# The opening of a two-layer decoder trunk: first loads in turns, the first chunk in four banks, TensorE on constants

## The chip, the cores and the metric

The kernel runs on one core of one Trainium2 chip, as one launch. The metric is the device time of that launch in microseconds (us). The kernel before takes 2181.18 us, the median of three runs (2179.99 to 2181.38).

A core has five engines that run their own instruction streams and meet at semaphores: TensorE (PE; its weight loads, PEld, are shown apart), VectorE (DVE), ScalarE (ACT), GpSimd (POOL) and SyncE (SP), which here only issues transfers. The transfers of all queues run on the same 16 DMA engines.

## The reference, cut to what matters

```python
DEPTH = 2; SEQ = 256; D_MODEL = 2048; PROJ_WIDTH = 6144
def reference(x, w_in, w_out, ...):
    for l in range(DEPTH):
        h = _rmsnorm(x, attn_norm_g[l])
        proj = h @ w_in[l]
        q, k, v, gate_b, gate_c, conv_in = jnp.split(proj, splits, axis=-1)
        q = _rmsnorm(q.reshape(B, S, N_HEADS, 2, HEAD_DK), q_norm_g[l])
        k = _rmsnorm(k.reshape(B, S, N_HEADS, 2, HEAD_DK), k_norm_g[l])
        ...
        attn = _diff_attention(q, k, v, lam, rel_bias)
        ...
        conv = gate_b * _short_conv(gate_c * conv_in, conv_w[l])
        x = x + jnp.concatenate([attn, conv.astype(attn.dtype)], axis=-1) @ w_out[l]
        hm = _rmsnorm(x, mlp_norm_g[l]) @ w_up[l]
        x = x + jnp.square(jax.nn.relu(hm)) @ w_down[l]
    return x
```

The change touches the first step of the first layer: x (256 rows of 2048) is loaded, turned, scaled by the gain of the norm, and multiplied with the first 512 columns of `w_in` (the first half of q). The row factor of the norm is applied later, to the product.

## The kernel before

**Numbers in two parts.** All large products are done in TensorE's reduced float32 (FP32R), with each operand split in two: a rounded high part (`hi`), made by ScalarE, and the rest (`lo`), made by VectorE from the original and the high part. Three products (high x high, high x low, low x high; `TERMS`, line 38) stand for one. So each weight tile that arrives as `raw` costs one ScalarE instruction (L282) and one VectorE instruction (L283) before TensorE can use it, and so does each piece of turned x (`split_gained`, L248 and L249, which also multiplies by the gain).

**Tiling.** x lies in four chunks `xs[n]` of 512 columns, each with both blocks of 128 rows. A chunk holds four K tiles of 128 columns. `Norm.chunk` turns a chunk with TensorE (L402): two banks of the accumulator memory, each with two K tiles of 256 rows, then four `split_gained` into the tile `nT`, then two squares on ScalarE with a running sum (L412), from which `Norm.factors` makes the row factors when all four chunks are ready. `linear` (L325) walks over 16 K tiles; for each it does six matmuls of 512 columns (two row blocks, three terms) against 512 columns of weights. Weights come two K tiles at a time, 512 KB, through four raw buffers and three buffers each for `hi` and `lo`.

**Order.** TensorE's instructions run in the order in which the program writes them (line 116). On the other engines a planner orders them by an estimated timeline, except those handed to `late` (line 118), which stay in program order. SP issues the loads of x (L136) and of the weights (L298). `Weights.take` makes the tiles up to three ahead of use (`AHEAD`, L313), and the planner decides where their roundings go.

**Background work.** `Background` (line 55) holds generators that are advanced one step by `work.tick()`, which `linear` calls after each K tile; a generator's `yield n` puts its next part n ticks later. So the transposes of the chunks, the attention of a half, the transposes of q and k (`qk_norm`, L478, 8 ticks after its product) and the loading of the bias are woven between the matmuls of the projections.

**The opening.** The gains are loaded on ScalarE's queue, then x chunk 0 in two halves on SP (line 143). The small vectors go over GpSimd's queue. `ident` is made on GpSimd, the gains are turned (L152), and chunk 0 is queued with no delay (line 992); its transposes come ahead of the first matmul, within one tick that `linear` gives while the chunk isn't ready. `first_loads` (line 986) issues two weight tiles and a chunk of x in turn and queues chunk n with 4n - 3 ticks, of which it waits for two more before its transposes. The first two weight tiles are rounded in two pieces each (`cut`, L280). Accumulator banks: three that turn under the tag `bank`, one `av`, and two double ones (`mm2`) for the products.

Of the kernel before, what the change touches and what calls it, by code (L numbers as in the profile page):

```python
# [9 lines left out]
F32 = mybir.dt.float32  # L10
F32R = mybir.dt.float32r
AF = mybir.ActivationFunctionType
# [3 lines left out]
P = 128  # L16
DEPTH = 2
D = 2048
S = 256
NT = S // P  # L20
AW = 1024
NH = 8
# [6 lines left out]
CH = 512  # L29
WC = 256  # L30
KG = 4
RAW = 4
AHEAD = 3
# [68 lines left out]
def trunk(ctx: ExitStack, tc: tile.TileContext, x, w_in, w_out, conv_w, q_norm_g, k_norm_g,  # L102
          lambda_q1, lambda_k1, lambda_q2, lambda_k2, subln_g, attn_norm_g, mlp_norm_g,
          w_up, w_down, rel_bias, selector, out):
    nc = tc.nc
    PSUM = bass.MemoryType.PSUM
    const = ctx.enter_context(tc.tile_pool(name="const", bufs=1))
# [4 lines left out]
    small = ctx.enter_context(tc.tile_pool(name="small", bufs=4))  # L112
    dram = ctx.enter_context(tc.tile_pool(name="dram", bufs=1, space=bass.MemoryType.DRAM))
    mm = ctx.enter_context(tc.tile_pool(name="mm", bufs=2, space=PSUM))
    ps = ctx.enter_context(tc.tile_pool(name="ps", bufs=3, space=PSUM))
    ctx.enter_context(tc.manual_schedule(engines={mybir.EngineType.PE}))

    def late(ins):

        tc.keep_in_program_order(ins)  # L120

    def bank(name):
        return ps.tile([P, CH], F32, tag="bank", name=name)
# [4 lines left out]
    work = Background()  # L128


    xs = [xpool.tile([P, NT, CH], F32, tag=f"x{n}", name=f"x{n}") for n in range(D // CH)]

    def load_x(n, cuts=1):
        for c in range(cuts):
            lo, hi = c * CH // cuts, (c + 1) * CH // cuts
            nc.sync.dma_start(  # L136
                xs[n][:, :, lo:hi],
                x[0, :, n * CH + lo:n * CH + hi].rearrange("(t p) c -> p t c", p=P))

    NG = DEPTH * D // P  # L140
    ngv = const.tile([NG, P], F32, tag="ngv", name="ngv")
    nc.scalar.dma_start(ngv, attn_norm_g.rearrange("l (k p) -> (l k) p", p=P))
    load_x(0, 2)

    ident = const.tile([P, P], F32, tag="ident", name="ident")
    make_identity(nc, ident)
    mhalf = const.tile([P, NH], F32, tag="mhalf", name="mhalf")
    nc.vector.memset(mhalf, -0.5)


    gps = bank("gps")
# [4 lines left out]
    def norm_gain(which, l, k):  # L156
        i = l * (D // P) + k
        return gains[:, MG + i:MG + i + 1] if which else ngains[:, i:i + 1]
# [19 lines left out]
    rel = const.tile([NB + 1, 2 * NH], F32, tag="rel", name="rel")  # L178
    nc.vector.memset(rel[NB:NB + 1, :], NEG)
    nc.gpsimd.dma_start(rel[0:NB, :], rel_bias)  # L180
    ones = const.tile([P, P], F32, tag="ones", name="ones")
    nc.vector.memset(ones, 1.0)

    gains = const.tile([P, ROWS], F32, tag="gains", name="gains")
    q_gain = const.tile([P, DEPTH], F32, tag="qg", name="q_gain")
    k_gain = gains[:, QG + DEPTH:QG + 2 * DEPTH]
# [59 lines left out]
    def split_gained(dst, k, src, gain):  # L246

        nc.scalar.activation(dst[:, 0, k], src, AF.Copy, scale=gain)  # L248
        nc.vector.scalar_tensor_tensor(  # L249
            dst[:, 1, k], src, gain, dst[:, 0, k].bitcast(F32), op0=ALU.mult, op1=ALU.subtract)  # L250
# [14 lines left out]
    class Weights:  # L265
# [5 lines left out]
            self.jobs, self.made, self.used = [], [], 0  # L271
            self.early = []

        def halves(self, raw, c=slice(None)):

            i = len(self.made)
            shape = [P] + list(raw.shape[1:])
            hi = wpool.tile(shape, F32R, tag="hi", name="whi")
            lo = wpool.tile(shape, F32R, tag="lo", name="wlo")
            first = self.cut and i < 2  # L280
            for k in (slice(0, 1), slice(1, None)) if first else (slice(None),):
                nc.scalar.activation(hi[:, k], raw[:, k], AF.Copy)  # L282
                nc.vector.tensor_sub(lo[:, k], raw[:, k], hi[:, k].bitcast(F32))  # L283
            return hi, lo

        cut = False

        def plain(self, w, row, c, nk):

            cols = 2 * CH // nk  # L290

            def make():
                raw = self.early.pop(0) if self.early else load()
                return self.halves(raw)

            def load():
                raw = self.pool.tile([P, nk, cols], F32, tag="raw", name="raw", bufs=RAW)
                nc.sync.dma_start(  # L298
                    raw, w[row:row + nk * P, c:c + cols].rearrange("(k p) c -> p k c", p=P))
                return raw  # L300

            make.load = load
            self.jobs.append(make)

        def load_early(self, n):

            for _ in range(n):
                self.early.append(self.jobs[len(self.early)].load())

        def take(self):  # L310
            i = self.used
            self.used += 1
            while len(self.made) < min(len(self.jobs), i + 1 + AHEAD):  # L313
                self.made.append(self.jobs[len(self.made)]())
            return self.made[i]

# [68 lines left out]
    class Norm:  # L385
# [2 lines left out]

        def __init__(self, which, l):
            self.which, self.l = which, l  # L390
            self.tiles = [Parts(apool, "a", f"nT{which}{l}_{n}") for n in range(D // CH)]
            self.ss = small.tile([P, NT, D // CH], F32, tag="ss", name=f"ss{which}{l}", bufs=2)

        def chunk(self, n, wait):
            yield wait
            a = self.tiles[n].open()
            for j in range(2):
                tp = bank(f"tpn{n}_{j}")
                for i in range(2):
                    k = 2 * j + i  # L400
                    for t in range(NT):
                        nc.tensor.transpose(  # L402
                            tp[:, i * S + t * P:i * S + (t + 1) * P],
                            xs[n][:, t, k * P:(k + 1) * P], ident)
                for i in range(2):
                    k = 2 * j + i
                    split_gained(a, k, tp[:, i * S:(i + 1) * S],
                                 norm_gain(self.which, self.l, n * KG + k))
            self.tiles[n].ready = True
            for t in range(NT):  # L410
                junk = wide(f"junk{n}_{t}")
                sq = nc.scalar.activation(junk, xs[n][:, t], AF.Square,  # L412
                                          accum_out=self.ss[:, t, n:n + 1])
                if (self.which, self.l) == (0, 0):
                    late(sq)

        def factors(self):
            while not all(t.ready for t in self.tiles):
                yield 1
            tot = small.tile([P, NT], F32, tag="tot", name="tot")  # L420
            nc.vector.tensor_reduce(tot, self.ss, axis=AX.X, op=ALU.add)
            r = rstd_of(tot, D, "row", NT)
            self.r = small.tile([P, NT], F32, tag="rowf", name="rowf", bufs=2)
            nc.vector.tensor_copy(self.r, r)
            diag = small.tile([P, NT, P], F32, tag="diag", name="diag", bufs=1)
            if self.which:

                self.scale = small.tile([P, 1], F32, tag="rowf2", name="rowf2")
                nc.vector.tensor_mul(self.scale, r[:, 1:2], r[:, 1:2])
                ratio = small.tile([P, 1], F32, tag="ratio", name="ratio")  # L430
                nc.vector.reciprocal(ratio, r[:, 1:2])
                nc.vector.tensor_mul(ratio, ratio, r[:, 0:1])
                nc.vector.tensor_scalar_mul(diag[:, 0], ident, ratio)
                yield 5
                tp = bank("rbc")
                nc.tensor.matmul(tp[:, :P], ones, diag[:, 0], start=True, stop=True)
                self.ratio = small.tile([P, P], F32, tag="rowb", name="ratiob", bufs=1)
                nc.vector.tensor_copy(self.ratio, tp[:, :P])
                return
            for t in range(NT):  # L440
                nc.vector.tensor_scalar_mul(diag[:, t], ident, self.r[:, t:t + 1])
            yield 5
            tp = bank("rbc")
            nc.tensor.matmul(tp[:, :S], ones, diag.rearrange("p t c -> p (t c)"),
                             start=True, stop=True)
            self.across = small.tile([P, 2, S], F32, tag="rowb", name="rowb", bufs=1)
            nc.vector.tensor_copy(self.across[:, 0], tp[:, :S])
            nc.gpsimd.tensor_tensor(self.across[:, 1], self.across[:, 0], self.across[:, 0],
                                    op=ALU.mult)
# [5 lines left out]
    def qk_norm(acc, r, dst, gain, name):  # L455

        out_ = []
        for t in range(NT):
# [6 lines left out]
            f = rstd_of(ms, DK, f"{name}{t}", NH)  # L465
# [5 lines left out]
                acc[:, t].rearrange("p (g d) -> p g d", d=DK),  # L471
                f2.unsqueeze(2).to_broadcast([P, NH, DK]), op=ALU.mult)
            out_.append(qn)
        yield 8
        for t in range(NT):
            tp = bank(f"{name}tp{t}")
            for i in range(4):
# [2 lines left out]
            hi, lo = (dst[:, i, :, t * P:(t + 1) * P] for i in range(2))  # L480
# [118 lines left out]
    def mixer(l, norm, loads):  # L599

        with ExitStack() as scope:
# [2 lines left out]
            rpool = scope.enter_context(tc.tile_pool(name="rpool", bufs=RAW))  # L604
            bpool = scope.enter_context(tc.tile_pool(name="bpool", bufs=8))
            weights = Weights(rpool)
            weights.cut = l == 0
            for half in range(2):
                for part in range(3):
                    weights.straight(w_in[l], 0, D // P, part * AW + half * CH)  # L610
# [373 lines left out]
    norm = Norm(0, 0)  # L984

    def first_loads(weights):
        for n in range(1, D // CH):
            weights.load_early(2)
            load_x(n)
            work.start(norm.chunk(n, 2), 4 * n - 3)  # L990

    work.start(norm.chunk(0, 0))
    for l in range(DEPTH):
        mnorm = mixer(l, norm, first_loads if l == 0 else lambda weights: None)
        norm = mlp(l, mnorm, l == DEPTH - 1)
# [31 lines left out]
```

## Time and profile before

| | before |
|---|---|
| median of three runs | 2181.18 us |
| profiled execution, its own time | 2181.14 us |
| its span, first to last instruction | 2179.4 us |
| TensorE busy | 2156.6 us (99%) |
| VectorE, ScalarE, GpSimd busy | 74%, 58%, 6% |
| read from memory | 425.84 MB, 204 GB/s over the span |
| first weights land | 8.32 us after the span's start |
| first matmul of the q projection | 9.90 us |

The profile is one execution, recorded by the hardware. "PE q L338 x12" in the chain of waits are twelve matmuls into the accumulator q from line 338. A wait row reads: engine, what it was about to write and its line, what released it; then the total, the number of times and the longest. A timeline row reads: start, busy time, engine, line, operation, output<-input, shapes, count, and in brackets the idle time before it and its releaser. Rows of merged instructions give their summed time. In the issue rows stand the size of a transfer and the microseconds from its issue to its landing; SPq is SP's queue. In the rows of windows each engine has its busy time and its instruction count; then follow the clock, the DMA engines' busy share and GB/s. The clock column of this profile stands at 1.00 from the first window on; the lengths of the matmuls tell more there.

### The profile page before, as it was taken

Reading aid. Unit: us, or ns where it says so; the run is one execution under the profiler, and the core shown is the slowest. Engines: PE = TensorE matmul, PEld = TensorE weight load, DVE = VectorE, ACT = ScalarE, POOL = GpSimd, SP = SyncE. Lnnn points to the kernel's source line nnn. Section 1 sums busy time; section 2 is a strip of 40 time slices with the busy share of each in tenths; the row PEclk is TensorE's granted clock in tenths of the full one; section 3 lists DMA queues with packets and bytes.
Section 4 is the critical chain, followed back from the end, with each engine's and each line's share of the span. In section 5 each row is a group of like instructions: output and inputs, shape, how many; then the busy total and the mean of one; then the engine's idle time right before and its main releaser. Section 6 shows DMA issues by size and latency. Waiting matters only on the chain.

```text
span 2179.4 us, 29050 instructions
## 1 busy us (share of the span) xinstructions
PE 2156.6 (99%) x11066; PEld 1828.6 (84%) x11066; DVE 1603.9 (74%) x2229; ACT 1271.7 (58%) x1718; POOL 138.8 (6%) x194
## 2 busy tenths in 40 slices
PE   8999999999999999999999999999999999999999
PEld 6888888888888888888888888888888888888887
DVE  6677655698888888855566776557988888887554
ACT  6456445566666666654454654455666666665443
POOL 2021100000000000100011111000000000001000
PEclk9999999999999999999999999999999999999999
DMA  7555656476666666587565466656766666666774
GB/s 256 180 156 177 218 185 184 157 238 223 213 212 215 220 208 214 189 277 241 175 205 181 156 199 197 184 173 190 225 218 217 213 212 216 219 208 212 246 242 145
DMA packets 292491, 446.62 MB, mean 205 GB/s; under 512 B 10403, under 2 KB 191221, under 8 KB 292352
## 3 DMA queue, kind: packets, MB, share of 16 engines
q1 hardware_dynamic: 285648, 423.66, 61.5%
q0 software_dynamic: 6656, 21.10, 2.6%
q8 instruction: 86, 1.41, 0.3%
q14 instruction: 53, 0.43, 0.1%
q10 hardware_dynamic: 48, 0.02, 0.0%
HBM read 425.84 MB, written 18.90 MB: 204 GB/s over the span
## 4 chain that ended last, share of the span: by engine, by line
PE 94%; DMA 2%; DVE 2%; ACT 1%; issue 1%; SPq 0%; DVEq 0%; ACTq 0%
PE upc L809 29%; PE dn L969 15%; PE pr L849 13%; PE o L338 8%; PE q L338 4%; PE gc L360 4%; PE ci L360 4%; PE k L338 4%; PE gb L360 4%; PE v L338 4%; PE upw L809 1%; DMA uraw<-in_w_up_dram 1%; PE sc L500 1%; PE av L536 1%; PE tpn L402 1%; DMA draw<-in_w_down_dram 1%
## 5 line engine op out<-in xcount | busy, mean ns | idle before, releaser
L283 DVE TENSOR_TENSOR wlo<-raw,whi 128x1024 fp32r<-128x1024 f32 (+1 forms) x386 | 473.3, 1228 | 385.5 <-ACT whi L282 381.0
L282 ACT ACTIVATE whi<-raw 128x1024 fp32r<-128x1024 f32 (+1 forms) x386 | 406.8, 1055 | 477.8 <-PE dn L969 166.7
L809 PE MATMUL upc<-nT,uhi 128*128 128x512 f32 x1920 | 477.5, 391 | 0.0
L694 ACT ACTIVATE uhi<-uraw 128x1024 fp32r<-128x1024 f32 x256 | 271.2, 1060 | 287.3 <-PE upc L809 253.9
L809 PEld LDWEIGHTS upc<-nT,uhi 128*128 128x128 f32 x1920 | 352.7, 188 | 68.2
L695 DVE TENSOR_TENSOR ulo<-uraw,uhi 128x1024 fp32r<-128x1024 f32 x256 | 312.8, 1222 | 115.3 <-ACT uhi L694 112.9
L969 PE MATMUL dn<-whi,g 128*128 128x512 f32 x1024 | 316.4, 389 | 0.0
L809 PEld LDWEIGHTS upc<-nT,ulo 128*128 128x128 f32 x1920 | 261.9, 190 | 18.7
L809 PE MATMUL upc<-nT,ulo 128*128 128x256 f32 x1920 | 267.7, 282 | 0.0
L969 PEld LDWEIGHTS dn<-whi,g 128*128 128x128 f32 x1024 | 192.2, 188 | 39.7
L969 PE MATMUL dn<-wlo,g 128*128 128x512 f32 x512 | 199.6, 390 | 1.1 <-DVE wlo L283 1.0
L338 PE MATMUL o<-whi,cat 128*128 128x512 f32 x512 | 159.6, 390 | 0.0
L969 PEld LDWEIGHTS dn<-wlo,g 128*128 128x128 f32 x512 | 96.1, 188 | 22.6 <-DVE wlo L283 2.8
L338 PEld LDWEIGHTS o<-whi,cat 128*128 128x128 f32 x512 | 96.2, 188 | 19.7
L338 PE MATMUL o<-wlo,cat 128*128 128x512 f32 x256 | 99.6, 389 | 0.0
L831 POOL DMA_DIRECT2D hid<-h x64 | 34.9, 545 | 949.1 <-ACT h L830 913.4
L849 PE MATMUL pr<-t13h,f 128*128 128x512 f32 x240 | 93.8, 391 | 0.0
L338 PE MATMUL q<-whi,nT 128*128 128x512 f32 x256 | 86.4, 406 | 4.1 <-ACT nT L248 4.1
L338 PE MATMUL k<-whi,nT 128*128 128x512 f32 x256 | 85.3, 399 | 0.0
L849 PE MATMUL pr<-t24h,f 128*128 128x512 f32 x240 | 84.0, 391 | 0.0
L849 PE MATMUL pr<-b2h,f 128*128 128x512 f32 x240 | 84.0, 391 | 0.0
L338 PE MATMUL v<-whi,nT 128*128 128x512 f32 x256 | 83.4, 396 | 0.0
(330 smaller groups left out, 3431.0 us busy)
## 6 DMA issues: line engine op xcount, KB each, us to landing
uraw<-in_w_up_dram SPq DMA_DIRECT2D x128, 1024.0 KB, 5.9
raw<-in_w_in_dram SPq DMA_DIRECT2D x192, 512.0 KB, 3.9
draw<-in_w_down_dram SPq DMA_DIRECT2D x64, 1024.0 KB, 5.1
raw<-in_w_down_dram SPq DMA_DIRECT2D x64, 1024.0 KB, 5.7
raw<-in_w_out_dram SPq DMA_DIRECT2D x64, 512.0 KB, 3.6
hid<-h POOLq DMA_DIRECT2D x64, 256.0 KB, 4.3
back<-hid SPq DMA_DIRECT2D x32, 512.0 KB, 3.3
rev<-by_dist_d POOLq DMA_DIRECT2D x4, 1024.0 KB, 11.1
```

What stands on the lines that cost most here:

```text
L282: nc.scalar.activation(hi[:, k], raw[:, k], AF.Copy)
L283: nc.vector.tensor_sub(lo[:, k], raw[:, k], hi[:, k].bitcast(F32))
L338: nc.tensor.matmul(acc[:, t], a.ap[:, pa, k % KG, t * P:(t + 1) * P], (hi, lo)[pw][:, j], start=(k == 0 and n == 0), stop=(k == nk - 1 and ...
L360: nc.tensor.matmul(acc[:, f, 0] if part else acc[:, f], wt[:, k % 4, fs], a.ap[:, 0, k % KG] if part else a.ap[:, :, k % KG], start=(part ...
L402: nc.tensor.transpose(tp[:, i * S + t * P:i * S + (t + 1) * P], xs[n][:, t, k * P:(k + 1) * P], ident)
L500: nc.tensor.matmul(sc[:, :W], qT[m * DK:(m + 1) * DK, a, i, t * P:(t + 1) * P], kT[m * DK:(m + 1) * DK, b, i, :W], start=(n == 0), stop=(n ...
L694: nc.scalar.activation(hi, src, AF.Copy)
L695: nc.vector.tensor_sub(lo, src, hi.bitcast(F32))
L809: nc.tensor.matmul(acc[:, 0] if part else acc, wt[:, k], a.ap[:, 0, k % KG] if part else a.ap[:, :, k % KG], start=(part == 0 and kh == 0 ...
L831: nc.gpsimd.dma_start(hid[i // 2][:, i % 2 * 2 * S:(i % 2 + 1) * 2 * S], u)
L849: nc.tensor.matmul(prods[n], fs[j][:, pa, a], b[pw], start=(j == 0 and m == 0), stop=(stop and m == 2))
L969: nc.tensor.matmul(acc[:, t], f[:, pa, k, t * P:(t + 1) * P], (hi, lo)[pw][:, k % 2], start=(b == 0 and k == 0 and m == 0), stop=(b == NB2 ...
```

## The change

The loads of x chunk 0 and of the first weight tile are issued in turns, a half of the chunk (two K tiles of x), one K tile of weights, the other half, the other K tile. Then come the second weight tile, x chunk 1, the third and fourth weight tiles, and x chunks 2 and 3. Chunk 0 is turned by a function of its own, `Norm.begin`: one bank for each of its four K tiles, the fourth under the tag `av`, and after the two parts of each K tile of x come the two parts of that K tile of weights, kept in program order. It runs at once, not in a tick. `ones` and `mhalf` are set first; 11 products of `ones` with itself go to TensorE ahead of the turning of the gains, and three more after the second and the fourth pair of transposes, into a bank that nobody reads. The squares of chunk 0 come six ticks later, those of chunks 1 and 2 three ticks later, and the factors wait for the squares. The first seven weight tiles are made with a shorter lead that grows (`ramp`), their roundings kept in program order. A small copy on ScalarE asks for its table at the start. Lastly `qk_norm` waits 10 ticks in place of 8, in both layers.

```diff
-    def load_x(n, cuts=1):
...
+    def load_x(n, lo=0, hi=CH):
+        nc.sync.dma_start(
+            xs[n][:, :, lo:hi],
+            x[0, :, n * CH + lo:n * CH + hi].rearrange("(t p) c -> p t c", p=P))
...
-    load_x(0, 2)
+    ones = const.tile([P, P], F32, tag="ones", name="ones")
+    nc.vector.memset(ones, 1.0)
+    mhalf = const.tile([P, NH], F32, tag="mhalf", name="mhalf")
+    nc.vector.memset(mhalf, -0.5)
+    started = small.tile([P, 1], F32, tag="started", name="started", bufs=1)
+    nc.scalar.activation(started, mhalf[:, 0:1], AF.Copy)
+    warm = mm.tile([P, NT, CH], F32, tag="mm2", name="warm")
+    def warm_up(n):
+        for _ in range(n):
+            nc.tensor.matmul(warm[:, 0, :P], ones, ones, start=True, stop=True)
     ident = const.tile([P, P], F32, tag="ident", name="ident")
     make_identity(nc, ident)
+    warm_up(11)
...
-        def halves(self, raw, c=slice(None)):
+        def halves(self, raw):
...
-            first = self.cut and i < 2
-            for k in (slice(0, 1), slice(1, None)) if first else (slice(None),):
-                nc.scalar.activation(hi[:, k], raw[:, k], AF.Copy)
-                nc.vector.tensor_sub(lo[:, k], raw[:, k], hi[:, k].bitcast(F32))
+            if not self.by_tile:
+                pair = (nc.scalar.activation(hi, raw, AF.Copy),
+                        nc.vector.tensor_sub(lo, raw, hi.bitcast(F32)))
+                if self.ramp and len(self.made) < 7:
+                    for ins in pair:
+                        late(ins)
             return hi, lo
...
+        def begin(self):
+            self.by_tile = self.ramp = True
+            raw = self.pool.tile([P, 2, CH], F32, tag="raw", name="raw", bufs=RAW)
+            w, row, c = self.first
+            for k in range(2):
+                load_x(0, k * CH // 2, (k + 1) * CH // 2)
+                nc.sync.dma_start(raw[:, k], w[row + k * P:row + (k + 1) * P, c:c + CH])
+            self.early.append(raw)
+            self.load_early(1)
+            raws = list(self.early)
+            self.made += [self.jobs[i]() for i in range(2)]
+            self.by_tile = False
+            def part(k):
+                (hi, lo), raw, j = self.made[k // 2], raws[k // 2], k % 2
+                late(nc.scalar.activation(hi[:, j], raw[:, j], AF.Copy))
+                late(nc.vector.tensor_sub(lo[:, j], raw[:, j], hi[:, j].bitcast(F32)))
+            return part
...
         def take(self):
...
-            while len(self.made) < min(len(self.jobs), i + 1 + AHEAD):
+            ahead = min(AHEAD, max(1, i - 2)) if self.ramp else AHEAD
+            while len(self.made) < min(len(self.jobs), i + 1 + ahead):
...
             self.tiles[n].ready = True
+            if (self.which, self.l) == (0, 0) and n < D // CH - 1:
+                yield 3
+            self.squares(n)
...
+        def begin(self, part):
+            a = self.tiles[0].open()
+            for k in range(KG):
+                tp = ps.tile([P, CH], F32, tag="av", name="tpb3", bufs=1) if k == KG - 1 else bank(f"tpb{k}")
+                for t in range(NT):
+                    nc.tensor.transpose(tp[:, t * P:(t + 1) * P],
+                                        xs[0][:, t, k * P:(k + 1) * P], ident)
+                if k % 2:
+                    warm_up(3)
+                split_gained(a, k, tp[:, :S], norm_gain(0, 0, k))
+                part(k)
+            self.tiles[0].ready = True
+            yield 6
+            self.squares(0)
+
         def factors(self):
-            while not all(t.ready for t in self.tiles):
+            while self.squared < D // CH:
...
-        yield 8
+        yield 10
...
     def first_loads(weights):
+        part = weights.begin()
         for n in range(1, D // CH):
-            weights.load_early(2)
             load_x(n)
+            if n == 1:
+                weights.load_early(2)
             work.start(norm.chunk(n, 2), 4 * n - 3)
-    work.start(norm.chunk(0, 0))
+        work.start(norm.begin(part))
```

More of the change, by code (lines that the diff above doesn't have):

```diff
@@ L131, in trunk @@
     xs = [xpool.tile([P, NT, CH], F32, tag=f"x{n}", name=f"x{n}") for n in range(D // CH)]
-    def load_x(n, cuts=1):
[L134 to L138, printed above, removed]
+    def load_x(n, lo=0, hi=CH):
+        nc.sync.dma_start(
+            xs[n][:, :, lo:hi],
+            x[0, :, n * CH + lo:n * CH + hi].rearrange("(t p) c -> p t c", p=P))
     NG = DEPTH * D // P
@@ L142, in trunk @@
     nc.scalar.dma_start(ngv, attn_norm_g.rearrange("l (k p) -> (l k) p", p=P))
-    load_x(0, 2)
+    ones = const.tile([P, P], F32, tag="ones", name="ones")
[8 more added lines that the diff above has]
+            nc.tensor.matmul(warm[:, 0, :P], ones, ones, start=True, stop=True)
     ident = const.tile([P, P], F32, tag="ident", name="ident")
     make_identity(nc, ident)
-    mhalf = const.tile([P, NH], F32, tag="mhalf", name="mhalf")
-    nc.vector.memset(mhalf, -0.5)
+    warm_up(11)
     gps = bank("gps")
@@ L180, in trunk @@
     nc.gpsimd.dma_start(rel[0:NB, :], rel_bias)
-    ones = const.tile([P, P], F32, tag="ones", name="ones")
-    nc.vector.memset(ones, 1.0)
     gains = const.tile([P, ROWS], F32, tag="gains", name="gains")
@@ L272, in __init__ @@
             self.early = []
-        def halves(self, raw, c=slice(None)):
-            i = len(self.made)
+        def halves(self, raw):
             shape = [P] + list(raw.shape[1:])
@@ L279, in halves @@
             lo = wpool.tile(shape, F32R, tag="lo", name="wlo")
-            first = self.cut and i < 2
-            for k in (slice(0, 1), slice(1, None)) if first else (slice(None),):
-                nc.scalar.activation(hi[:, k], raw[:, k], AF.Copy)
-                nc.vector.tensor_sub(lo[:, k], raw[:, k], hi[:, k].bitcast(F32))
-            return hi, lo
-        cut = False
+            if not self.by_tile:
[4 more added lines that the diff above has]
+                        late(ins)
+            return hi, lo
+        by_tile = ramp = False
+        def begin(self):
[15 more added lines that the diff above has]
+            return part
         def plain(self, w, row, c, nk):
@@ L302, in plain @@
             make.load = load
+            if not self.jobs:
+                self.first = w, row, c
             self.jobs.append(make)
@@ L307, in load_early @@
             for _ in range(n):
-                self.early.append(self.jobs[len(self.early)].load())
+                self.early.append(self.jobs[len(self.made) + len(self.early)].load())
         def take(self):
@@ L390, in __init__ @@
             self.which, self.l = which, l
+            self.squared = 0
             self.tiles = [Parts(apool, "a", f"nT{which}{l}_{n}") for n in range(D // CH)]
@@ L409, in chunk, with squares @@
             self.tiles[n].ready = True
+            if (self.which, self.l) == (0, 0) and n < D // CH - 1:
+                yield 3
+            self.squares(n)
+        def squares(self, n):
+            self.squared += 1
             for t in range(NT):
@@ L606, in mixer @@
             weights = Weights(rpool)
-            weights.cut = l == 0
             for half in range(2):
```

## The prediction

> **What bounds the kernel now.** I read the page first, then the waits of TensorE, then the chain of waits at its start, then the first microseconds of the timeline.
>
> ```profile
> span 2179.4 us, 29050 instructions
> PE 2156.6 (99%) x11066; PEld 1828.6 (84%) x11066; DVE 1603.9 (74%) x2229; ACT 1271.7 (58%) x1718; POOL 138.8 (6%) x194
> ...
> PE q L338 <- ACT nT L248: 4.1, 1, 4.1
> PE gps L152 <- POOL ident masks.py:199: 3.5, 1, 3.5
> PE up L809 <- ACT ev L819: 3.2, 2, 2.0
> ```
>
> TensorE is busy for 2156.6 of 2179.4 us, and its order is written by hand, so the time is its stream plus its waits. The two largest single waits, 3.5 and 4.1 us, lie before the first projection matmul; no other wait is over 2.0. The change can win in the opening only.
>
> ```profile
> 1.72 6.60 DMA raw<-in_w_in_dram
> ...
> 8.34 0.03 ACT whi L282
> ...
> 8.88 0.61 ACT whi L282
> 9.49 0.37 ACT nT L248
> ...
> 9.90 5.49 PE q L338 x12
> 15.39 1.15 PE tpn L402 x8
> 16.54 5.49 PE q L338 x24
> 22.03 0.87 PE tpn L402 x8
> ...
> 27.75 1.59 PE q L338 x6
> ```
>
> The chain at the start (start, length, what) says three things. The first projection matmul starts at 9.90, because ScalarE sat on the first weights (landed 8.32) before it rounded activations that had long been there. From 9.90 the matmuls run at half speed: 12 take 5.49, later 24 take 5.49; the 8 transposes 1.15, later 0.87. So the slow clock costs 5.49/2 + 0.28 = 3.0 us, and the full clock came 5.5 to 6.6 us after 9.90. And K tile 4 (six matmuls to a K tile) starts at 16.54 + 2.74 = 19.28: this is my yardstick, since from there on the stream has hardly a gap (0.22 at 27.75, where 6 took 1.59 against 1.37).
>
> **The change part by part.**
>
> Constants on TensorE. A float32 product with `ones` is two instructions. Nothing in the trace is just this; the nearest row is the broadcast of the row factors:
>
> ```profile
> 37.64 0.43 PE rbc L444 x2
> ...
> 1.21 1.28 ACT L282 ACT_TABLE_LOAD   x1 [1.21 <-PEq L1012]
> ...
> 0.80 0.07 DVE L148 MEMSET mhalf<- 128x8 f32 x1 [0.80 <-PEq L1012]
> ...
> 1.04 0.17 DVE L182 MEMSET ones<- 128x128 f32 x1
> ...
> 3.50 0.31 PE L152 MATMUL gps<-ident,ngv 32*128 32x32 f32 x1 [3.50 <-POOL ident masks.py:199]
> 3.81 2.01 PE L402 MATMUL tpn<-ident,x 128*128 128x128 f32 x8
> ```
>
> 0.43 for 256 columns warm gives 0.215 for 128 warm and 0.43 cold. `ones` becomes VectorE's first instruction (0.80 + 0.17), so TensorE starts at about 1.1 instead of 3.50. In order, cold: 11 constants 4.73 (to 5.83), the gains' transpose 0.31 (6.14), four transposes 0.58 (6.72), three constants 1.29 (8.0), four transposes, three constants. The gains' transpose and the chunk's wait for nothing now: ident was ready by 3.44, the first half of x by 3.7 (below). If the full clock comes 5.5 to 6.6 us after continuous work begins, as above, it comes at 6.6 to 7.7. With 6.6: the four transposes end at 6.7, the constants at 7.3, the transposes (half of 0.87) at 7.75, the last constants at 8.4. With 7.7: 8.95. [...]
>
> [...]
>
> First loads in turns. SP issues x half, K tile 0, x half, K tile 1, then weights 2/3, x chunk 1, and the rest: the bytes before any later transfer are the same, one issue more (0.47).
>
> ```profile
> 0.72 0.95 SPq L136 DMA_DIRECT2D x<-in_x_dram  x2
> ...
> 1.72 0.98 SPq L298 DMA_DIRECT2D raw<-in_w_in_dram  x2
> 2.74 0.47 SPq L136 DMA_DIRECT2D x<-in_x_dram  x1
> ...
> x<-in_x_dram SPq DMA_DIRECT2D x1, 256.0 KB, 3.0
> ...
> raw<-in_w_in_dram SPq DMA_DIRECT2D x1, 512.0 KB, 7.4
> x<-in_x_dram SPq DMA_DIRECT2D x1, 512.0 KB, 8.4
> ...
> raw<-in_w_in_dram SPq DMA_DIRECT2D x1, 512.0 KB, 9.1
> ...
> 5.00:10.00 5.00, 0.91 (x5) 0.51 (x3) 1.00 (x2) 1.66 (x4) 2.37 (x5) 1.00 0.99 333
> 10.00:15.00 5.00, 5.00 (x12) 3.78 (x13) 3.89 (x8) 4.14 (x10) 1.05 (x2) 1.00 1.06 386
> ```
>
> These rows (issues with microseconds to landing, and windows with the DMA share last but one) give landings of 3.7 for the first half of x, 2.23 + 7.4 = 9.6 for the second weights, 2.74 + 8.4 = 11.1 for x chunk 1, 3.25 + 9.1 = 12.35 for the third weights. The DMA engines are full from 5 to 15 (0.99, 1.06), so the extra issue is covered by the backlog; without it, it costs 0.47. K tile 1 now ends where the first weights ended, so I keep 8.3 for it; K tile 0 lies between 3.7 and 8.3, and I take 5.5. Four opening transfers could also land later than two large ones; a whole issue, 0.5, is my bound.
>
> Rounding in turns. Per K tile ScalarE has one part of the chunk and one of the weights, VectorE the same:
>
> ```profile
> 8.34 1.15 ACT L282 ACTIVATE whi<-raw 128x512 fp32r<-128x512 f32 x2 [5.85 <-DMA raw<-in_w_in_dram]
> 9.00 1.29 DVE L283 TENSOR_TENSOR wlo<-raw,whi 128x512 fp32r<-128x512 f32 x2 [4.96 <-ACT whi L282]
> 9.40 0.82 ACT L248 ACTIVATE nT<-tpn,ngains 128x256 fp32r<-128x256 f32 x2
> ...
> 10.21 0.87 DVE L249 SCALAR_TENSOR_TENSOR nT<-tpn,ngains,nT 128x256 fp32r<-128x256 f32 x2
> ...
> 13.08 1.06 ACT L282 ACTIVATE whi<-raw 128x1024 fp32r<-128x1024 f32 x1
> 14.18 1.23 DVE L283 TENSOR_TENSOR wlo<-raw,whi 128x1024 fp32r<-128x1024 f32 x1 [1.11 <-ACT whi L282]
> ```
>
> So 0.58 + 0.41 = 0.99 on ScalarE and 0.65 + 0.44 = 1.09 on VectorE, under TensorE's 1.37 (5.49/4) for a K tile. K tile 0 is rounded by about 8.0; K tile 1 has its high part at 8.9 and its low part at 9.6, needed at 8.4 + 1.37 + 0.23 = 10.0; the second weights give tile 2 at 10.2 and 10.9, needed from 11.1; tile 3 at 11.9, needed after 12.5. All fit, by 0.2 to 0.5. The third weights, landed 12.35, are rounded high at 13.4 and low at 14.6: K tile 4 cannot run before 14.4. The wait that goes is therefore followed closely by this one.
>
> Four banks instead of two, with the fourth in the "av" bank that no one uses yet, cost nothing: the three turning banks are held by the gains and two tiles only. ScalarE's table load (1.21 to 2.49) is only asked for by an instruction of its own now and stays ahead of every landing.
>
> The new order on ScalarE and VectorE has one wait that holds others up: K tile 1's weights (8.3), behind which the parts of tiles 2 and 3 are queued; TensorE, still on constants and tile 0 until 9.8, doesn't ask for them before 11.1.
>
> Sum. TensorE does K tiles 0 to 3 (5.49) and chunk 1's transposes (0.87) after its start at 8.4: K tile 4 at 14.8 in place of 19.28, a gain of 4.5; with the clock at 7.7, 3.9; with the data as the bound (14.4), 4.9. The squares, put off, leave ScalarE freer in this stretch; I add 0.15, most of the gap at 27.75. Gain 4.65: 2179.4 - 4.65 = 2174.75 of span, and the profiled run had 2181.14, 1.74 outside the span, so 2176.5. That run stands at the median (2181.18), nothing is corrected.
>
> The squares moved back 3 or 6 steps are queued behind nothing on TensorE; the factors now wait for them, but chunk 3's squares stay where they are, so r comes no later.
>
> The turned q and k (yield 10 for 8), at eight places:
>
> ```profile
> 123.33 0.60 PE L478 MATMUL q01tp<-ident,q01n 128*128 128x128 f32 x4
> ...
> 125.27 1.25 ACT L481 ACTIVATE qT<-q01tp,q_gain 128x512 fp32r<-128x512 f32 x2
> ...
> 125.97 0.75 DVE L482 SCALAR_TENSOR_TENSOR qT<-q01tp,q_gain,qT 128x512 fp32r<-128x512 f32 x1
> ...
> 128.49 0.55 PE sc L500 x6
> ```
>
> They wait on nothing at TensorE now, so no gain. Two K tiles later, q's two transposes come one K tile before and together with the scores, which take two of the three banks. A bank was held from 123.33 to 125.97 + 0.75 = 126.72, 3.4 us. That is the price where they collide; nothing is the other bound, and I take nothing, because each user leaves at least 1.37 us to the next.
>
> **The rivals.**
>
> Chunks 1 to 3 come late. The old opening spent one step on chunk 0, so chunk n's transposes stood two K tiles before their use, and now one. For: chunk 2's transposes began at 22.03 and VectorE's first low part of it only ended at 24.85 (below); the cover is 0.87 + 1.37 + 0.46 = 2.7 against 2.8 taken. Against: the weights' rounding is now kept behind. Stalls of 0.5 to 1.0 at three chunks: 2178.0 to 2179.5.
>
> ```profile
> 24.42 0.86 DVE L249 SCALAR_TENSOR_TENSOR nT<-tpn,ngains,nT 128x256 fp32r<-128x256 f32 x2
> ```
>
> The constants don't lift the clock, or fill TensorE too long. Cold throughout, the opening ends at 1.1 + 17 x 0.43 + 0.31 + 1.15 = 9.9, where it was: 2181. Against: matmuls are matmuls.
>
> Banks collide after the turned q and k (slower). In the second half of both layers q and k are turned while scores run: four places, 3.4 each at most, 13.6 - 4.65 = 9 us slower, 2190. It decides from 4.65/4 = 1.2 us a place, and is over the bound below from 2.25. For: three banks, and a shift by half the period of the scores. Against: the rows show spare time before and after.
>
> **How the numbers follow.** A measurement of this kernel tells about 0.2%, 4.4 us, from no change. Forecast 0.62, its own range 2175.4 to 2177.6; late chunks 0.16; clock or constants 0.08; banks 0.14. The forecast straddles 2176.8, the bound; I give it 0.57 for faster, as the clock, the one term with a wide spread, can come earlier than 6.6 but was not seen later than 7.7; the rest of it and the next two cases make 0.29 for the same, the banks 0.14 slower. The range goes from 2175.0 (data bound and another 0.9) to 2181.5, which leaves out the banks.
>
> **What would show it.** First projection matmul at 8 to 9 and the first 12 in under 3.3 us; K tile 4 at 14.4 to 15.4; constants at 0.43, then 0.22; the first weights' two landings at about 5.5 and 8.3; no wait of TensorE on nT at chunks 1 to 3 above 0.3; no new wait at q01tp or the scores behind it. I am wrong if the first matmul starts after 10 or the 12 still take 5.5 (clock), if K tile 4 is reached by 15 and the end does not follow (stalls later), or if TensorE waits for banks near 126.

## The result and the profile after

| | before | after |
|---|---|---|
| median of 6 runs each (us) | 2180.59 | 2196.51 |
| lowest to highest | 2179.09 to 2181.88 | 2194.96 to 2197.14 |
| ratio, 95% interval | | 1.0072 [1.0059, 1.0085] |
| profiled execution, its span | 2181.14, 2179.4 | 2196.17, 2194.4 |

The kernel became slower by 15.9 us (0.72%). The forecast was 2176.5, and its range ended at 2181.5.

The opening came out as the prediction drew it. From the timeline of TensorE in the profile of after (start, length, instruction):

```profile
1.04 5.06 PE L153 MATMUL warm<-ones 128*128 128x128 f32 x22 [1.04 <-DVE mhalf L145]
...
6.83 0.83 PE L153 MATMUL warm<-ones 128*128 128x128 f32 x6
...
8.53 0.47 PE L370 MATMUL q<-whi,nT 128*128 128x512 f32 x1
...
11.14 0.62 PE L370 MATMUL q<-whi,nT 128*128 128x512 f32 x2
...
14.76 0.61 PE L370 MATMUL q<-whi,nT 128*128 128x512 f32 x2
```

The 11 constants (22 instructions) take 0.46 each, the next three (0.83) 0.28 each; counted to the start of the next instruction, that is 0.45 (1.04 to 6.03) and 0.22 (6.83 to 7.50), so what the prediction calls the slow clock ends between them. The first projection matmul starts at 8.53, and the twelfth is the first of the pair at 11.14. The second matmul of the last row, at 14.76 + 0.23 = 14.99, is the first of K tile 4. In the same view of before it is the second of this row, at 18.92 + 0.23 = 19.15 (the prediction's 19.28 was added up from the chain):

```profile
18.92 0.62 PE L338 MATMUL q<-whi,nT 128*128 128x512 f32 x2
```

Then the lead goes. The table takes the first matmul of some products from the timelines of both profiles:

| first matmul of | before | after | after - before |
|---|---|---|---|
| k, layer 1 | 39.31 | 36.76 | -2.55 |
| o, layer 1 | 310.18 | 308.37 | -1.81 |
| up, layer 1 | 399.97 | 400.57 | +0.60 |
| dn, layer 1 | 918.74 | 920.73 | +1.99 |
| q, layer 2 | 1096.81 | 1103.39 | +6.58 |
| o, layer 2 | 1390.84 | 1398.05 | +7.21 |
| up, layer 2 | 1480.62 | 1490.25 | +9.63 |
| dn, layer 2 | 1999.18 | 2009.05 | +9.87 |
| end of the span | 2179.4 | 2194.4 | +15.0 |

More than half of the loss arises behind the first matmul of dn, 4.6 us in layer 1 and 5.1 in layer 2, and another 2.4 in each layer from o to up, all of it far from what the diff touches. From q to o of layer 2 only 0.6 is lost. No wait explains this: in the list of TensorE's waits after, the largest behind the opening was there before (3.2 then), and the new ones are small.

```profile
PE up L863 <- ACT ev L873: 3.0, 2, 1.6
...
PE q01tp L533 <- DVE qT L537: 0.7, 1, 0.7
PE q11tp L533 <- DVE qT L537: 0.7, 1, 0.7
...
PE q L370 <- DVE nT L255: 0.6, 1, 0.6
```

What grew is TensorE's busy time, from 2156.6 to 2176.7; 6.7 of the 20.1 are the constants. The groups of the page (busy time, mean ns of one) name the place, first before, then after:

```profile
L969 PE MATMUL dn<-whi,g 128*128 128x512 f32 x1024 | 316.4, 389 | 0.0
...
L338 PE MATMUL o<-whi,cat 128*128 128x512 f32 x512 | 159.6, 390 | 0.0
...
L338 PE MATMUL k<-whi,nT 128*128 128x512 f32 x256 | 85.3, 399 | 0.0
```

```profile
PE 2176.7 (99%) x11100; PEld 1831.5 (83%) x11100; DVE 1604.3 (73%) x2229; ACT 1271.7 (58%) x1719; POOL 139.1 (6%) x194
...
L1023 PE MATMUL dn<-whi,g 128*128 128x512 f32 x1024 | 323.0, 396 | 0.0
L370 PE MATMUL o<-whi,cat 128*128 128x512 f32 x512 | 162.8, 396 | 0.0
...
L370 PE MATMUL k<-whi,nT 128*128 128x512 f32 x256 | 85.4, 399 | 0.0
```

Each matmul of o and dn is 6 to 7 ns longer, while those of k are as they were. The chain of waits gives it more finely, as one piece of it holds 576 matmuls of dn without a gap, before and after:

```profile
957.33 130.58 PE dn L969 x576
```

```profile
959.90 134.39 PE dn L1023 x576
```

That is 130.58/576 = 226.7 ns from start to start, and 134.39/576 = 233.3. The sources of these loops are the same in both kernels, and so are their instructions.

### The profile page after: what moved, and what is told of

Read it like the earlier page. It is cut to its first block, busy times and chain, and to the rows that moved or that the text cites. A ratio compares the mean times of both kernels' runs of the same rounds, so it can differ in the third digit from the quotient of the medians.

```text
span 2194.4 us, 29124 instructions
## 1 busy us (share of the span) xinstructions
PE 2176.7 (99%) x11100; PEld 1831.5 (83%) x11100; DVE 1604.3 (73%) x2229; ACT 1271.7 (58%) x1719; POOL 139.1 (6%) x194
## 4 chain that ended last, share of the span: by engine, by line
PE 93%; DVE 3%; DMA 3%; ACT 1%; issue 1%; DVEq 0%; ACTq 0%
PE upc L863 29%; PE dn L1023 16%; PE pr L903 12%; PE o L370 8%; PE gc L392 4%; PE ci L392 4%; PE gb L392 4%; PE v L370 4%; PE k L370 4%; PE q L370 4%; DMA uraw<-in_w_up_dram 1%; PE upw L863 1%; PE sc L555 1%; PE av L591 1%; DVE ulo L749 1%
## 5 line engine op out<-in xcount | busy, mean ns | idle before, releaser
L287 DVE TENSOR_TENSOR wlo<-raw,whi 128x1024 fp32r<-128x1024 f32 x382 | 471.7, 1237 | 394.8 <-ACT whi L286 394.0
L286 ACT ACTIVATE whi<-raw 128x1024 fp32r<-128x1024 f32 x382 | 403.9, 1059 | 481.7 <-PE dn L1023 176.1
L1023 PE MATMUL dn<-whi,g 128*128 128x512 f32 x1024 | 323.0, 396 | 0.0
```

The lines of the kernel that those rows point to most:

```text
L286: pair = (nc.scalar.activation(hi, raw, AF.Copy), nc.vector.tensor_sub(lo, raw, hi.bitcast(F32)))
L287: nc.vector.tensor_sub(lo, raw, hi.bitcast(F32)))
L1023: nc.tensor.matmul(acc[:, t], f[:, pa, k, t * P:(t + 1) * P], (hi, lo)[pw][:, k % 2], start=(b == 0 and k == 0 and m == 0), stop=(b == NB2 ...
```

## The experiments

Each ratio below is to before, run again beside that experiment; the traces are of one execution each.

Two theories stood against each other, and one beside them. **Places**: the small copy on ScalarE writes to a tile, `started`, that takes 32 bytes of each partition in the pool `small`. That pool lies ahead of those of `cat`, `g`, `f`, `kT`, `qT` and behind those of `nT`, `whi`, `wlo`, so that the first now lie 32 bytes further against the second; by this theory the matmul of a stationary operand (128 columns, in the trace the 128x128 that PEld loads, 188 ns each for dn) from one side with a moving one (the 512 columns) from the other is slower. **Work**: something that the change does (its transfers, its orders, the constants) slows TensorE later on. **Banks** was the prediction's slower rival, at the turned q and k.

**1. After without the copy and its tile.**

```diff
-    started = small.tile([P, 1], F32, tag="started", name="started", bufs=1)
-    nc.scalar.activation(started, mhalf[:, 0:1], AF.Copy)
```

> The changed kernel without the small tile 'started' and the copy that fills it; all else stays. That tile takes 32 bytes in the pool 'small' and moves every pool behind it (cat, g, f, raw) by 32 bytes against the pools ahead of it (nT, the rounded weights). Theory, the shift: matmuls of o and dn (one operand behind the tile, one ahead) took 233.3 ns from start to start instead of 226.7 of the kernel before, some 16 us in all; here they go back to 226.7 and the time to 2179 to 2181.5. Rival, the banks or the turned q and k two ticks later: the time stays at 2196. Rival, the 34 more TensorE instructions change how its stream is fetched: stays at 2196.

2181.97 us (2179.13 to 2183.35, 10 runs), ratio to before 1.0007 [0.9998, 1.0017]. The loss is gone. The piece of dn in its chain:

```profile
957.89 130.59 PE dn L1021 x576
```

That leaves open whether it was the copy or its tile. The next two settle that from the other side.

**2 and 3. Before with an unused tile of 32 or of 64 bytes, and nothing else of the change.**

```diff
+    pad = small.tile([P, 8], F32, tag="pad", name="pad", bufs=1)
+    nc.vector.memset(pad, 0.0)
```

(the second with `[P, 16]`)

> The kernel before with one unused tile of 32 bytes in the pool 'small', set once by VectorE; nothing else of the change. Theory, the shift: o and dn at 233.3 ns, upc up by 1.5, pr down by 2; 2196 to 2197.5. Every rival: 2180.6, as before, since nothing else is changed.

> The same with a tile of 64 bytes. If what counts is the place of the two operands modulo 64 bytes: 2180.6, o and dn at 226.7. If it is any move of the later pools, or their place modulo more than 64 bytes: slower than 2185.

2195.59 us (2193.89 to 2196.67), ratio 1.0070 [1.0055, 1.0085], and 2197.97 (2197.40 to 2198.62), ratio 1.0082 [1.0067, 1.0097]. The two chains:

```profile
958.29 134.40 PE dn L971 x576
```

```profile
962.14 134.40 PE dn L971 x576
```

An unused tile in the old kernel costs as much as the whole change did, with the same 233.3 ns. So it is places, not work. The shift of 64 bytes is as bad as that of 32, so a period of 64 is out.

**4. After with the turned q and k as before** (`yield 8` for 10, line 529).

```diff
-        yield 10
+        yield 8
```

> The changed kernel with 8 ticks instead of 10 ahead of the turned q and k; 'started' stays. Theory, the shift: only the two waits of 0.7 us at q01tp and q11tp go, 2195. The predicted slower rival (banks that collide after the turned q and k): the loss goes, 2176 to 2181.

2196.67 us (2196.33 to 2197.03), ratio 1.0075 [1.0058, 1.0092]. The two waits of 0.7 go, but another comes, at the first of the turned tiles:

```profile
PE q00tp L533 <- DVE q00n L524: 1.6, 1, 1.6
```

That is a wait for the input `q00n`, not for a bank. Banks cost 1.4 us at most and were traded for 1.6. As the cause of the loss this rival falls; as a mechanism it was there, in small.

**5. The matmul by itself.** The computation is left out, and one execution was recorded: 31 groups of 48 FP32R matmuls, `A` stationary (128 columns), `B` moving (512 columns), both tiles at multiples of 4096 bytes, and the start of one or both shifted by d and e bytes.

```diff
+        for n in range(48):
+            a = d // 4 + n % 4 * P
+            b = e // 4 + n % 2 * 512
+            nc.tensor.matmul(acc, A[:, a:a + P], B[:, b:b + 512], start=(n == 0), stop=(n == 47))
```

> A kernel that leaves the whole computation out: it stores x, and in between runs 31 groups of 48 rounded float32 matmuls of 512 columns, back to back, from two tiles that both start at a multiple of 4096 bytes. In each group the stationary slices, the moving slices or both are moved by a number of bytes (0 to 2048). Theory, the two places against each other: 226.7 ns from start to start where both are moved alike or by a large power of two, about 233 where they differ by 32 or 64 bytes. Rival, the place of one operand alone: both moved by 32 is as slow as one. Rival, traffic of the other engines in the full kernel decides: all groups equal.

The chain lists the groups one after the other; a length is that of 48 matmuls with the end of the last. In the first fence the stationary operand alone is shifted, by 16, 32, 64, 128, 192, 256, 384 and 1024 bytes:

```profile
27.77 11.48 PE sab L42 x48
...
40.02 11.47 PE sac L42 x48
...
64.50 11.47 PE sae L42 x48
...
89.03 11.44 PE sag L42 x48
...
113.50 11.29 PE sai L42 x48
...
137.81 11.21 PE sak L42 x48
...
149.79 11.44 PE sal L42 x48
...
173.95 11.21 PE san L42 x48
```

In the second, the moving one alone by 32, 64 and 256, then both by 32, both by 64, the two by 32 and 64, by 64 and 32, and neither:

```profile
210.10 11.48 PE saq L42 x48
...
222.35 11.28 PE sar L42 x48
...
258.89 11.19 PE sau L42 x48
...
294.85 11.21 PE sax L42 x48
...
306.83 11.21 PE say L42 x48
...
342.76 11.48 PE sbb L42 x48
...
355.00 11.48 PE sbc L42 x48
...
379.21 11.23 PE sbe L42 x48
```

From start to start, behind the first eight of each group, the fast groups take 226.7 to 227.0 ns, the slow ones up to 234.4; shifted by 192 (stationary) or 64 (moving), which is the same difference modulo 256, they take 228.9. So what counts is neither place by itself but the one against the other, and only modulo 256 bytes: alike is fast, everything else that was tried is slower by 2 to 8 ns of 227.

**6 and 7. After, with the copy kept and the shift taken away in two ways.** First `started` goes into the pool `const`, the first of all, so that all the large pools move by 32 bytes together; then it shares a slot of `small` that is there anyway, so that none moves.

```diff
-    started = small.tile([P, 1], F32, tag="started", name="started", bufs=1)
+    started = const.tile([P, 1], F32, tag="started", name="started")
```

```diff
-    started = small.tile([P, 1], F32, tag="started", name="started", bufs=1)
+    started = small.tile([P, 1], F32, tag="c", name="started")
```

> The changed kernel with 'started' in the pool 'const', ahead of x, nT and the rounded weights: the same instructions, and now all pools with large tiles move by 32 bytes together. Theory, the two places against each other: o and dn back at 226.7, 2178 to 2182. Rival, the place of the later pools by itself: as slow as the changed kernel, 2196.

> The changed kernel with 'started' in a buffer that 'small' has anyway (tag c): the same instructions, no pool moves. What is left is the change without the shift. If the predicted gain of the opening is real and stays: 2176 to 2178. If the later stages give it back (two waits of 0.7 us at q01tp and q11tp, the start of the feed-forward part bound by its loads): 2179 to 2181.

2180.51 us (2178.92 to 2182.96, 10 runs), ratio 1.0002 [0.9993, 1.0012], and 2180.33 (2178.88 to 2183.56, 11 runs), ratio 1.0002 [0.9993, 1.0010]. The chains:

```profile
957.76 130.59 PE dn L1023 x576
```

```profile
955.48 130.59 PE dn L1023 x576
```

With every instruction of the change in place, the matmuls are fast again, even where all places differ from before by 32 bytes. The shift of one side against the other is the cause of the loss. But the change without it is not faster than before either, which the last three follow up.

**8. As 7, with the wait of 10 only at the first turned tile** (line 529; the others 8), since the wait of 1.6 in experiment 4 arose there and the two of 0.7 elsewhere.

```diff
-        yield 10
+        yield 10 if name == "q00" else 8
```

> The same, and 10 ticks ahead of the turned tiles only for the first q of the first layer, where 8 cost a wait of 1.6 us in the run with 8 everywhere; 8 elsewhere. The two waits of 0.7 us should go: 1 to 1.5 us under the run before this one. If they only move what waits at the start of the feed-forward part: no difference.

2179.07 us (2177.00 to 2180.49, 11 runs), ratio 0.9994 [0.9986, 1.0003]. All three waits are gone from TensorE's list; the time isn't told from before's.

**9. As 8, with chunks 2 and 3 begun a step earlier.**

```diff
-            work.start(norm.chunk(n, 2), 4 * n - 3)
+            work.start(norm.chunk(n, 2), 4 * n - (3 if n == 1 else 4))
```

> The unshifted kernel with one 10, and x chunks 2 and 3 turned one K tile earlier (4n - 4 ticks for n of 2 and 3), so that two K tiles lie between their transposes and their use, as in the kernel before. If late chunks cost the opening its rest (waits of 0.6 on DVE nT and 0.3 on DVE wlo, some 1 us of stream): 1 us under the run with one 10, 2178. If the weights' rounding is the limit there: no difference.

2182.05 us (2179.37 to 2187.32, 11 runs), ratio 1.0009 [1.0000, 1.0018]. A miss: the stall at chunk 3 was to go, and instead the first matmul of k came at 39.56, behind before's 39.31, with new waits of TensorE:

```profile
PE rbc L499 <- DVE diag L496: 2.2, 1, 2.2
...
PE q L370 <- ACT whi L286: 1.0, 1, 1.0
PE q L370 <- DVE wlo L287: 0.8, 1, 0.8
```

An earlier turn moved more than the turn: the row factors came later. The chain of this run names the place:

```profile
29.71 3.16 DMA by_dist_d<-by_dist
...
33.16 1.84 POOL rev L241 x2
...
35.08 0.92 POOL row_e L412
```

GpSimd now issued the loads of the bias (`rev`), which wait for the transfer `by_dist_d`, ahead of the first step of the row factors, `row_e`. That step started at 35.08, against 32.34 in experiment 8, though its input was ready earlier (31.57 against 31.97). Whether an earlier chunk helps when that order is kept was not tried.

**10. As 8, without the constants** (line 152).

```diff
-        for _ in range(n):
+        for _ in range(0):
```

> The unshifted kernel with one 10 and no constants on TensorE at all (neither the 11 nor the 6). If the constants give what the prediction put on them, the first 12 matmuls take 5.1 to 5.5 us instead of 2.8 and k starts 1.5 to 3 us later: 2180.5 to 2182. If the first matmul then starts a microsecond earlier, because the six no longer stand in its way, half of that: 2179.5 to 2180.5. Rival, the loads set the pace of the first four K tiles anyway: 2179.

2177.89 us (2175.81 to 2179.94, 11 runs), ratio 0.9987 [0.9978, 0.9996]. It is the only version whose interval lies below 1, 3.0 us under the 2180.92 of before beside it. Its timeline:

```profile
7.85 0.78 PE L370 MATMUL q<-whi,nT 128*128 128x512 f32 x1
8.43 0.63 PE L370 MATMUL q<-wlo,nT 128*128 128x512 f32 x1
...
10.00 0.63 PE L370 MATMUL q<-whi,nT 128*128 128x512 f32 x2
...
10.69 0.62 PE L370 MATMUL q<-whi,nT 128*128 128x512 f32 x2
```

The run to compare with is experiment 8, which differs by the constants alone. The first projection matmul comes no sooner without them (7.85, against 7.89 there). From 10.00 on six matmuls go in 1.37, at the full clock, so only some five are slow. K tile 4 starts 0.9 later than in experiment 8 (15.21 against 14.35), k only 0.3 later (36.58 against 36.32): some 0.6 of the constants' lead goes where TensorE, in experiment 8, waits for the low part of the fourth weight tile, a wait that this run doesn't have. In the time the constants bought nothing that was measured; whether leaving them out gains is open, as the interval overlaps that of experiment 8.

## Why the prediction was wrong

**The failed step is the cost of the table copy.** The prediction said: "ScalarE's table load (1.21 to 2.49) is only asked for by an instruction of its own now and stays ahead of every landing." It put the copy at nothing. That is right of the instruction (0.2 us at 2.50 in the timeline of after, behind nothing), but its output was not counted. The tile for that output is what moved `cat`, `g` and `f` against the weights. Worked out from the pools' order and sizes, `cat` began at byte 171872 of a partition and the first buffer of `whi` at 74592; the difference, 97280, is 380 times 256. After, `cat` is at 171904, the difference 32 bytes more. The sum is then

| matmuls, both layers | number | ns each, before | after | us |
|---|---|---|---|---|
| o | 768 | 226.9 | 233.3 | +4.9 |
| dn | 1536 | 226.8 | 233.3 | +10.0 |
| `pr` of the rounded weights (line 989) | 96 | 227.2 | 233.4 | +0.6 |
| `upc`, 512 columns | 1920 | 228.4 | 229.9 | +2.9 |
| `pr` of the other factors (line 903), another such next | 1140 | 229.6 | 227.8 | -2.1 |
| the same, `upc` next | 120 | 226.8 | 234.8 | +1.0 |

with steps from start to start counted over the trace, those with a wait left out: 17.3 us, beside 16.8 that the table of first matmuls shows from o of layer 1 (-1.81) to the end (+15.0). The first three rows, 15.5 us, are the products with one operand on either side of `small`. The projections q, k and v, whose operands both lie in pools ahead of `small`, are unchanged, as the row of k showed.

The other rows are not explained by the place of a product's own two operands: `upc` has both ahead of `small`, line 903 both behind it. They do hang on the tile, as `upc` is back at 228.4 in experiments 1, 6 and 7. The last row would fit if what counts is the moving operand against the weights that are loaded meanwhile for the next matmul (before, the load for the second matmul of dn runs from 918.74 to 918.93, the first matmul from 918.74 to 919.13), which for `upc` lie ahead; no run tests that, and why `upc` and the rest of line 903 change stays open.

**The terms of the opening held.** The first projection matmul was forecast at 8.4 and came at 8.53; K tile 4 at 14.8 and came at 14.99; the constants at 0.43 cold, measured 0.46; the clock was to come at 6.6 or 7.7, and the three constants from 6.83 on took 0.28 each; the first 12 projection matmuls were to take under 3.3, and took 2.84 (8.53 to 11.37 in the timeline). By the timelines of both, K tile 4 came 4.2 sooner, of 4.5 forecast. The constants' part in it was small: 0.9 by experiments 8 and 10, where the slow clock was put at 3.0, as without them the matmuls are at their full rate from 10.00 on (six in 1.37). That the clock "can come earlier than 6.6", on which the prediction leaned for its chance of faster, no row of before shows; in the chain of experiment 1 the 11 constants take 4.44 from 1.04 on, against 5.06 after, and the gains' transpose behind them 0.19, against 0.24, so there it came before 5.48.

**The gain did not reach k: a second step that failed.** There it was 2.55. The sum ended at K tile 4, "since from there on the stream has hardly a gap". That was read off before; after, from K tile 4 to k, takes 21.77 us where before takes 20.16. The rival "chunks come late" held at one chunk of three, the last. From the timeline of after:

```profile
17.48 0.61 PE L370 MATMUL q<-whi,nT 128*128 128x512 f32 x2
...
18.29 0.50 PE L370 MATMUL q<-wlo,nT 128*128 128x512 f32 x1 [0.19 <-DVE wlo L287]
...
30.33 1.02 PE L370 MATMUL q<-whi,nT 128*128 128x512 f32 x2
...
30.47 1.23 DVE L287 TENSOR_TENSOR wlo<-raw,whi 128x1024 fp32r<-128x1024 f32 x1 [1.38 <-ACT whi L286]
...
31.19 0.39 PE L370 MATMUL q<-wlo,nT 128*128 128x512 f32 x1
...
31.61 0.87 DVE L255 SCALAR_TENSOR_TENSOR nT<-tpn,ngains,nT 128x256 fp32r<-128x256 f32 x2
32.14 0.73 PE L370 MATMUL q<-whi,nT 128*128 128x512 f32 x2 [0.56 <-DVE nT L255]
```

VectorE had the weights' low part ahead of chunk 3's own, and TensorE waited 0.6 us for it. From start to start the step there is 0.95 (31.19 to 32.14) in place of 0.23, and the step before it, behind chunk 3's high part, 0.52 (30.33 to 30.85). With the next matmul after each, some 0.1 longer, chunk 3 costs 1.2, over the 0.5 to 1.0 that the rival named for a chunk. The other 0.5 goes at the low part of the fourth weight tile (17.71 to 18.29, and the next), for which the prediction gave no landing. Together that is 1.7, beside the 1.6 between the two stretches.

**The yardstick was one draw.** The prediction measured the gain against K tile 4 at 19.28, which hangs on a first projection matmul at 9.90 in the one profiled execution. The old opening stands unchanged in experiments 2 and 3, and there its first weights landed after 4.88 or 6.64 us:

```profile
1.72 4.88 DMA raw<-in_w_in_dram
```

```profile
1.72 6.64 DMA raw<-in_w_in_dram
```

In experiment 2 q starts at 8.18 and k at 36.96, only 0.2 behind after's 36.76. In experiment 3 k starts at 39.47, near before's 39.31. So the old opening itself reaches k some 2.4 us earlier or later, by when one transfer lands, and the gain of 2.55 is against a late draw. That fits experiments 6, 7 and 8, which keep the new opening and are not told from before. Behind the opening a lead changes too: in the profile of experiment 7 it is 2.2 us at o of layer 1, 1.8 at dn, 1.1 at o of layer 2 and 0.4 at the end; in that of experiment 10 it is 2.5, 3.3, 3.4 and 4.1. What moves it, and how often the old landing is early, stays open, as a profile shows one execution.

**Banks.** "They wait on nothing at TensorE now" was right of before, but not of the opening moved forward: with 8 ticks `q00tp` then waits 1.6, for its input. With 10, two places collide at 0.7 each, well under the 1.2 a place from which this rival was to decide.

## What to carry to other kernels

A new tile can have a price even where its instruction is hidden, as it moves every pool behind it: here 32 bytes cost the kernel before 15.6 us (2195.59 beside 2179.96, experiment 2). Before a small change is costed, list which operands of the long matmul loops lie on either side of the tile, and keep their difference a multiple of 256 bytes where they are of the kind tried here (FP32R, 512 columns; 226.7 to 227.0 ns so, 228.9 to 234.4 for the others tried in experiment 5), by sharing a slot or by putting the tile ahead of both. When busy time grows and waits don't, compare the mean duration of the same instruction group in both profiles before looking for a stall; and take a landing time as a range from several executions (here 4.88 to 6.64), not as one number.

## What was not expected of the hardware

The pairs of a weight load and a 512-column matmul in FP32R, by themselves in experiment 5, run at 226.7 to 227.0 ns when the starts of both operands agree modulo 256 bytes, and at 228.9 to 234.4 for the other differences tried, from 16 bytes on. What in the chip does this was not found out. A first load of 512 KB, issued at 1.72 in the same way, took 4.88 or 6.64 us to land. And the granted clock reads 1.00 in the first 40 us of before and after, while matmuls in it run at half their speed (before, 12 take 5.49 from 9.90 on and 24 take 5.49 from 16.54 on): that this is a slow clock is the author's reading of the lengths, which that column doesn't show.
